# Four instead of three pairs of k-tiles by seven products in the second part's down projections

## The chip, the cores and the metric

The program runs on one core of one Trainium2 chip. The metric is the device time of one execution in microseconds (us). The kernel before has a median of 1944.74 us over 3 runs (1944.4 to 1944.83). A kernel's trace is one further execution, taken by the hardware profiler.

## The reference: one decoder block, of which the two feed-forward networks matter here

```python
def swiglu(x, w_gu, w_down):
    gate, up = jnp.split(x @ w_gu, 2, axis=-1)
    return (jax.nn.silu(gate) * up) @ w_down

h = h + 0.5 * swiglu(rms_norm(h, ffn1_norm[i]), ffn1_w_gu[i], ffn1_w_down[i])
...                                    # the mixer: input projection, DeltaNet, attention, output projection
h = h + 0.5 * swiglu(rms_norm(h, ffn2_norm[i]), ffn2_w_gu[i], ffn2_w_down[i])
...                                    # per-layer embedding, last norm
```

There are 256 tokens (two row tiles of 128, called t = 0 and 1), a model width of 2048 and a hidden width of 5632, all in float32, one layer.

## The kernel before, in words

**Exactness by two halves.** Every float32 operand is split into a rounded part and a rest: ScalarE casts (`whi`, `shi`, `hTh`), VectorE subtracts (`wlo`, `slo`, `hTl`). One product is then three matmuls on TensorE: hi·hi, lo·hi, hi·lo. A 128x512 block of weights for one k-tile and one row tile thus takes three matmuls.

**Parts and groups.** The hidden width is 11 blocks of 512, cut by `PARTS` into a first part of 3 blocks and a second and a third part of 4. For each part the kernel runs one gate/up group per block and then two down groups (`dn`, `nb` = 0 and 2), each of which makes two column blocks of 512 of the down projection. A down group of the second part has 8 pairs of k-tiles in each of its two column blocks. The groups of one feed-forward network are a fixed list (`plan`), and there are two such networks: the first fills the first third of the trace, the second its last two fifths.

**Two ways of multiplying.** In a group some pairs of k-tiles go the plain way: a weight pair is loaded (L74, 512 KB), cast (`whi`, L77), subtracted (`wlo`, L78) and used by 12 matmuls (L550 to L552). The other pairs, `ns` of them for each column block, are multiplied by a Winograd form of Strassen's scheme: the four quarters (two k-tiles by two column blocks) need seven products instead of eight. The class `Group` does this. A quarter is a tile `R` of 128 x (ns·512), loaded by `load` (L279, GpSimd's DMA queue). `all_sums` makes the seven right-hand sides in turn: cast `shi` from `R` (L298, ScalarE), subtract to `slo` (L299, VectorE), and between them add quarters into `R` (L307 on VectorE, or L314, a DMA that adds). `product` uses each with 3·ns matmuls (L342 to L344). I call the seven products of a group p1 to p7, in the order in which they run. After p1 and p2 ScalarE copies the sum to another bank (L347); after p3 and p5 it copies their bank aside (L350) for a VectorE subtraction (L352).

**Buffers.** `shi` and `slo` have two buffers each, `whi` and `wlo` three, `raw` four. The cast of p3 therefore waits until p1 has been multiplied, that of p4 until p2 has been, and so on; a `whi` waits for the pair three before it.

**The left-hand sides.** Four of the seven products use sums of row tiles and k-tiles of the activations. `halves` makes them: for each pair of k-tiles an addition (L456), four additions or subtractions of quarters (L462), a cast `Sh` (L464) and a subtraction `Sl` (L465). In a part after the first it takes one pair at a time, as the hidden blocks come out of `down_input` (which transposes them by way of DRAM).

**What sets the order.** The seven products of a group stand among the plain pairs of the group before it: after one or two plain pairs, one product after each further pair. So the products of the second part's first down group (D1 below) stand in that part's last gate/up group, those of the second down group (D2) among D1's plain pairs, and those of the next gate/up group (ns = 4) among D2's. Within these lists a scheduler orders the instructions of each engine when the program is built; each engine then runs its own list in that order.

**What the change touches:** `NS_DOWN` (L31) with `plan`, `halves`, `ffn` and the weights' layout.

Of the kernel before, what the change touches and what calls it, by code (L numbers as in the profile page):

```python
# [26 lines left out]
PARTS = ((0, 3), (3, 7), (7, 11))  # L27


NS = 4  # L30
NS_DOWN = tuple(3 if i1 - i0 == 4 else 2 for i0, i1 in PARTS)  # L31


SEVEN = (0, 1, 2, 4, 3, 5, 6)
# [12 lines left out]
def block_kernel(ctx, tc, a, out):  # L47
# [306 lines left out]
    def plan(n):  # L354


        def sources(name, blk):

            q, pairs = a[name + "q"][blk], a[name][blk]
            return [q[:, :, g, :].rearrange("j p n -> p j n") for g in range(q.shape[2])] + \  # L360
                [pairs[g] for g in range(pairs.shape[0])], q

        groups = []
        for p, (i0, i1) in enumerate(PARTS):
            for i in range(i0, i1):
                plain = PLAIN[n]
                if i < plain:
                    src = [([a[f"w_gu{n}0"][2 * i + b][g] for g in range(KD // 2)], None) for b in range(2)]
                else:
                    src = [sources("w_gu" + n, 2 * (i - plain) + b) for b in range(2)]  # L370
                groups.append(Group("gu", p, [x[0] for x in src], [x[1] for x in src], NS if i >= plain else 0,
                                    len(groups) % 2))
            for nb in (0, 2):
                src = [sources(f"w_down{n}{p}", nb + b) for b in range(2)]
                groups.append(Group("dn", p, [x[0] for x in src], [x[1] for x in src], NS_DOWN[p], len(groups) % 2, nb))
        if n == "2":
            src = [sources("w_behind", b) for b in range(2)]
            groups.append(Group("behind", len(PARTS), [x[0] for x in src], [x[1] for x in src], NS_BEHIND,
                                len(groups) % 2))
        if n == "1":  # L380

            groups[0].plain.sort(key=lambda x: x[1])
        made, carried = [], []
        for i, group in enumerate(groups):
            group.follower = follower = groups[i + 1] if i + 1 < len(groups) else None
            after = groups[i + 2] if i + 2 < len(groups) else None
            n_plain = len(group.plain)
            at, loads, carried = [], {0: carried}, []
            if follower is not None and follower.ns:
                first = 8 if not group.ns else 4 if follower.kind == "behind" else \  # L390
                    1 if group.kind == follower.kind or group.part and follower.kind == "dn" else 2
                at = [min(first + j, n_plain - 1) for j in range(7)]
                if not group.ns:
                    follower.first = n

                    loads.setdefault(max(at[0] - 5, 0), []).extend(follower.loads())
                if after is not None and after.ns:
                    *three, last = after.loads(follower)
                    for x, one in zip((4, 5, 6), three):
                        loads.setdefault(at[x], []).append(one)  # L400
                    carried = [last]
            todo = []
            for j, (b, g) in enumerate(group.plain):
                todo.append(("plain", (b, g)))
                order.append(("pair", group.src[b][g]))
                if group.kind == "behind" and g == KD // 2 - 1:
                    order.append(("pair", a["w_pp"][b]))
                for x in range(7):
                    if at and at[x] == j:
                        todo.append(("seventh", x))  # L410
                        order.append(("sum", follower))
                order.extend(loads.get(j, []))
            made.append((group, todo))
        return made
# [8 lines left out]
    def halves(kind, his, los, ns, wait=0, at_once=2):  # L423
# [19 lines left out]
        for g0 in range(0, ns, at_once):  # L443
            n = min(at_once, ns - g0)
            k0 = 2 * (g0 % 2)
            hi, lo = (x[g0 // 2][:, k0:k0 + 2 * n] for x in (his, los))
            keep = lambda ins: ins
            if g0 == 2 and n == 1:

                keep = tc.keep_in_program_order  # L450
                yield
            if n == 2:
                x = fp.tile([P, 2 * NB], F32, tag="sil", name="S")
            else:
                x = act.tile([P, NB], F32, tag="nat", name="S", bufs=4)
            keep(nc.vector.tensor_tensor(out=x, in0=hi.bitcast(F32).rearrange("p k x -> p (k x)"),  # L456
                                         in1=lo.bitcast(F32).rearrange("p k x -> p (k x)"), op=ALU.add))
            xv = x.rearrange("p (g j t y) -> p g j t y", g=n, j=2, t=2)
            a11, a12, a21, a22 = (xv[:, :, j, t, :] for t in range(2) for j in range(2))
            for o, y, z, op in ((a22, a21, a22, ALU.subtract), (a21, a11, a21, ALU.subtract),  # L460
                                (a11, a22, a11, ALU.subtract), (a12, a11, a12, ALU.add)):
                nc.vector.tensor_tensor(out=o, in0=y, in1=z, op=op)  # L462
            sx = [y[:, g0:g0 + n].rearrange("p g j t y -> p (g j t y)") for y in (sh, sl)]
            nc.scalar.copy(sx[0], x)  # L464
            nc.vector.tensor_tensor(out=sx[1], in0=x, in1=sx[0], op=ALU.subtract)  # L465
            if not g0 % 2 + n == 1 or g0 + n == ns:
                yield

    def ffn(n, nT, r, scale, next_norm, stat):
        xs = picker(*nT)  # L470
        late = callable(r)
        with tc.tile_pool(name="ffn", bufs=1) as fp:
# [43 lines left out]
            for group, todo in ffn_plan[n]:  # L516
# [5 lines left out]
                if dn and group.nb and not group.last:  # L522
                    lanes.add(1, halves("gu", *nT, NS))
                elif dn and group.nb and group.follower:
                    lanes.add(1, halves("behind", *nxt, NS_BEHIND, 4))
                elif not dn and group.follower.kind == "dn" and not group.part:
                    lanes.add(1, halves("dn", hTh[i0:], hTl[i0:], NS_DOWN[group.part]))
                if dn and group.last and nxt is None:
                    nxt = new_nT()
                if group.banks is None:  # L530
# [1 line left out]
                for kind, one in todo:  # L532
                    if kind == "seventh":
                        follower = group.follower
                        follower.product(SEVEN[one])
                        if group.part and not dn and one == 5 and follower.kind == "gu" and \
                                follower.follower.kind == "dn":
                            p = PARTS[group.part][0]
                            lanes.add(1, halves("dn", Later(hTh, p), Later(hTl, p), NS_DOWN[group.part], 0, 1))
                        continue  # L540
                    b, g = one
                    whi, wlo = next_weights()
# [29 lines left out]
                    else:  # L572
# [7 lines left out]
                        hTl.append(tl)  # L580
                        i0, i1 = PARTS[group.part]

                        last = (3 if i1 - i0 == 4 else 2) if len(hTh) == i1 else 0
                        gen = down_input(outs, sil, th, tl, last)
                        next(gen)

# [762 lines left out]
def _layout(i):  # L1349
# [7 lines left out]
    for n in "12":  # L1357
# [4 lines left out]
        _parted(m, f"w_gu{n}", b[2 * PLAIN[n]:], NS)  # L1362
        b = _blocks(f[f"ffn{n}_w_down"][0])
        for p, (i0, i1) in enumerate(PARTS):
            _parted(m, f"w_down{n}{p}", b[:, 2 * i0:2 * i1], NS_DOWN[p])
    _parted(m, "w_behind", _blocks(f["ple_w_gate"][0])[0:2], NS_BEHIND)
    w = f["w_in"][0]
    m["w_in"] = _blocks(np.concatenate([w[:, :4096], w[:, 4112:]], axis=1))
# [29 lines left out]
```

## Time and profile before

| | |
|---|---|
| median of 3 runs | 1944.74 us |
| profiled execution | 1945.28 us |
| its span, first to last instruction | 1943.6 us |
| mean granted TensorE clock | 0.999 |
| matmuls in the trace | 8884 |
| busy share of the span | TensorE 99%, VectorE 81%, ScalarE 60%, GpSimd 8% |
| a quarter of the second part's down weights | 768 KB, 7.0 us from issue to landing |
| a quarter of the gate/up weights | 1024 KB, 8.3 us |

Times in the trace are counted from the span's start. In lists of groups the columns are the line, the engine, the operation, output and inputs with their shapes, the count, then busy us and mean ns of one, then the idle time of the engine before them with what ended it. In a timeline a row has its start in us, its duration in us, the engine, the line and the operation; an idle time in brackets is the engine's own, and names what ended it. PE is TensorE, PEld its weight loads, DVE VectorE, ACT ScalarE, POOL GpSimd.

### The profile page before, as it was taken

To read this page: it belongs to the slowest core of one execution; us is meant where nothing else is said; L and a number is where in the kernel's file an instruction comes from. 1 tells how busy PE (TensorE), PEld (TensorE's weight loads), DVE (VectorE), ACT (ScalarE), POOL (GpSimd) and SP (SyncE) were. 2 spreads that over 40 slices of the span, in tenths; PEclk is the share of its full clock that TensorE was granted. 3 is DMA by queue.
4 is the path that set the end of the run, shared out by engine and by line. 5 is a ranking of instruction groups with operands and counts; after the bars stand their busy time and mean duration, and the time that the engine had idled before them with its cause. 6 is when DMAs were issued, how large, how long until landed. Compare 5 with 4: busy or idle time off the path is not lost.

```text
span 1943.6 us, 24163 instructions
## 1 busy us (share of the span) xinstructions
PE 1928.1 (99%) x8884; PEld 1594.0 (82%) x8884; DVE 1570.4 (81%) x1703; ACT 1164.1 (60%) x1362; POOL 148.4 (8%) x226
## 2 busy tenths in 40 slices
PE   9999999999999999999999999999999999999998
PEld 7888888888888888878788888888888888888886
DVE  7879878997789766797856579899888987888865
ACT  6656666666666557664555456566556755657654
POOL 0010110000010000010100000010000100001000
PEclk9999999999999999999999999999999999999999
DMA  8778898888888765556565776788888987989764
GB/s 307 269 236 282 252 293 285 237 288 249 280 285 242 228 218 171 176 169 211 161 213 159 244 283 231 226 281 289 248 275 241 327 264 244 271 237 314 234 214 143
DMA packets 144182, 475.05 MB, mean 244 GB/s; under 512 B 19648, under 2 KB 47296, under 8 KB 129856
## 3 DMA queue, kind: packets, MB, share of 16 engines
q1 hardware_dynamic: 107200, 302.16, 44.4%
q0 software_dynamic: 25920, 160.44, 30.2%
q10 hardware_dynamic: 10944, 10.91, 1.8%
q8 instruction: 69, 1.13, 0.2%
q14 instruction: 49, 0.40, 0.1%
HBM read 451.44 MB, written 22.02 MB: 244 GB/s over the span
## 4 chain that ended last, share of the span: by engine, by line
PE 92%; DVE 5%; DMA 2%; issue 1%; ACT 0%; POOL 0%; SPq 0%; POOLq 0%; DVEq 0%; ACTq 0%
PE d L550 5%; PE d L552 5%; PE d L551 5%; PE u L551 5%; PE u L552 5%; PE u L550 5%; PE g L343 5%; PE g L342 5%; PE g L344 5%; PE g L551 4%; PE g L552 4%; PE pj L112 4%; PE pj L113 4%; PE pj L114 4%; PE g L550 4%; PE d L344 3%
## 5 line engine op out<-in xcount | busy, mean ns | idle before, releaser
L77 ACT CAST whi<-raw 128x1024 fp32r<-128x1024 f32 (+1 forms) x489 | 511.3, 1049 | 401.1 <-PE pj L114 106.6
L78 DVE TENSOR_TENSOR wlo<-raw,whi 128x1024 fp32r<-128x1024 f32 (+1 forms) x489 | 592.0, 1218 | 162.9 <-ACT whi L77 161.8
L299 DVE TENSOR_TENSOR slo<-R,shi 128x2048 fp32r<-128x2048 f32 (+2 forms) x224 | 444.9, 1989 | 132.1 <-ACT shi L298 130.1
L298 ACT CAST shi<-R 128x2048 fp32r<-128x2048 f32 (+2 forms) x224 | 373.9, 1671 | 141.5 <-DVE R L307 62.7
L112 PE MATMUL pj<-whi,nTh 128*128 128x512 f32 x448 | 179.4, 401 | 0.0
L113 PE MATMUL pj<-wlo,nTh 128*128 128x512 f32 x448 | 175.2, 391 | 1.1 <-DVE wlo L78 1.1
L114 PE MATMUL pj<-whi,nTl 128*128 128x512 f32 x448 | 174.9, 390 | 0.0
L550 PE MATMUL d<-whi,hTh 128*128 128x512 f32 x448 | 174.5, 390 | 0.0
L551 PE MATMUL d<-wlo,hTh 128*128 128x512 f32 x448 | 174.4, 389 | 0.0
L552 PE MATMUL d<-whi,hTl 128*128 128x512 f32 x448 | 173.4, 389 | 0.0
L551 PE MATMUL g<-wlo,nTh 128*128 128x512 f32 x400 | 156.6, 391 | 0.6 <-DVE wlo L78 0.6
L552 PE MATMUL g<-whi,nTl 128*128 128x512 f32 x400 | 156.0, 390 | 0.0
L551 PE MATMUL u<-wlo,nTh 128*128 128x512 f32 x400 | 155.8, 389 | 0.2 <-DVE wlo L78 0.2
L552 PE MATMUL u<-whi,nTl 128*128 128x512 f32 x400 | 155.6, 389 | 0.0
L550 PE MATMUL g<-whi,nTh 128*128 128x512 f32 x400 | 155.0, 391 | 0.6 <-ACT nTh L161 0.6
L550 PE MATMUL u<-whi,nTh 128*128 128x512 f32 x400 | 153.4, 389 | 0.0
L307 DVE TENSOR_TENSOR R<-R 128x2048 f32<-128x2048 f32 (+2 forms) x68 | 135.7, 1996 | 0.1
L113 PEld LDWEIGHTS pj<-wlo,nTh 128*128 128x128 f32 x448 | 84.2, 188 | 18.9 <-DVE wlo L78 2.7
L550 PEld LDWEIGHTS d<-whi,hTh 128*128 128x128 f32 x448 | 84.1, 188 | 18.1 <-ACT hTh L504 1.0
L552 PEld LDWEIGHTS d<-whi,hTl 128*128 128x128 f32 x448 | 84.1, 188 | 17.8
L114 PEld LDWEIGHTS pj<-whi,nTl 128*128 128x128 f32 x448 | 84.1, 188 | 17.6
L551 PEld LDWEIGHTS d<-wlo,hTh 128*128 128x128 f32 x448 | 84.1, 188 | 17.4
(332 smaller groups left out, 3447.0 us busy)
## 6 DMA issues: line engine op xcount, KB each, us to landing
raw<-in_w_gu SPq DMA_DIRECT2D x199, 512.0 KB, 5.8
raw<-in_w_down SPq DMA_DIRECT2D x112, 512.0 KB, 6.4
raw<-in_w_in SPq DMA_DIRECT2D x112, 512.0 KB, 3.4
R<-in_w_gu2q POOLq DMA_DIRECT2D x54, 1024.0 KB, 8.6
R<-in_w_gu1q POOLq DMA_DIRECT2D x48, 1024.0 KB, 8.3
raw<-in_w_out SPq DMA_DIRECT2D x32, 512.0 KB, 4.3
tT<-scr SPq DMA_DIRECT2D x22, 512.0 KB, 5.8
R<-in_w_down11q POOLq DMA_DIRECT2D x12, 768.0 KB, 7.0
```

The source lines that it names most:

```text
L77: nc.scalar.copy(hi[:, j, :], raw[:, j, :])
L78: nc.vector.tensor_tensor(out=lo[:, j, :], in0=raw[:, j, :], in1=hi[:, j, :], op=ALU.subtract)
L112: nc.tensor.matmul(outs[t], xh[:, c], whi[:, j, :], start=st, stop=False)
L113: nc.tensor.matmul(outs[t], xh[:, c], wlo[:, j, :], start=False, stop=False)
L114: nc.tensor.matmul(outs[t], xl[:, c], whi[:, j, :], start=False, stop=sp)
L298: keep(nc.scalar.copy(hi, w))
L299: nc.vector.tensor_tensor(out=lo, in0=w, in1=hi, op=ALU.subtract)
L307: keep(nc.vector.tensor_tensor(out=self.raw[x], in0=self.raw[x], in1=self.raw[y], op=ALU.add))
L344: nc.tensor.matmul(out, xl, whi[:, g, :], start=False, stop=sp, skip_group_check=True)
L550: nc.tensor.matmul(out, xh[:, c], whi[:, j, :], start=st, stop=False, skip_group_check=True)
L551: nc.tensor.matmul(out, xh[:, c], wlo[:, j, :], start=False, stop=False, skip_group_check=True)
L552: nc.tensor.matmul(out, xl[:, c], whi[:, j, :], start=False, stop=sp, skip_group_check=True)
```

## The change

Each of the four down groups of the second part (two in each network) takes 4 instead of 3 pairs by seven products, and 4 instead of 5 of each column block the plain way. The first part stays at 2, the third at 3. The table now has one entry for each of a part's two down groups, and each has its own weight tensors.

```diff
-NS_DOWN = tuple(3 if i1 - i0 == 4 else 2 for i0, i1 in PARTS)
+NS_DOWN = (2, 2), (4, 4), (3, 3)
...
             for nb in (0, 2):
-                src = [sources(f"w_down{n}{p}", nb + b) for b in range(2)]
-                groups.append(Group("dn", p, [x[0] for x in src], [x[1] for x in src], NS_DOWN[p], len(groups) % 2, nb))
+                src = [sources(f"w_down{n}{p}{nb // 2}", b) for b in range(2)]
+                groups.append(Group("dn", p, [x[0] for x in src], [x[1] for x in src], NS_DOWN[p][nb // 2],
+                                    len(groups) % 2, nb))
...
-            if g0 == 2 and n == 1:
+            if g0 >= 2 and n == 1:
 
                 keep = tc.keep_in_program_order
-                yield
+                if g0 == 2:
+                    yield
...
-                    lanes.add(1, halves("dn", hTh[i0:], hTl[i0:], NS_DOWN[group.part]))
+                    lanes.add(1, halves("dn", hTh[i0:], hTl[i0:], NS_DOWN[group.part][0]))
...
-                            lanes.add(1, halves("dn", Later(hTh, p), Later(hTl, p), NS_DOWN[group.part], 0, 1))
+                            lanes.add(1, halves("dn", Later(hTh, p), Later(hTl, p), NS_DOWN[group.part][0], 0, 1))
...
-                        last = (3 if i1 - i0 == 4 else 2) if len(hTh) == i1 else 0
+                        last = (6 - NS_DOWN[group.part][0] if i1 - i0 == 4 else 2) if len(hTh) == i1 else 0
...
-            _parted(m, f"w_down{n}{p}", b[:, 2 * i0:2 * i1], NS_DOWN[p])
+            for j in range(2):
+                _parted(m, f"w_down{n}{p}{j}", b[2 * j:2 * j + 2, 2 * i0:2 * i1], NS_DOWN[p][j])
```

The scheduler's order moves with it. In the changed kernel, lines after L375 count one to three higher. Numbers behind a name are those of a tile's allocation; a tile that is the same in both programs need not have the same number.

The first place is VectorE in the last gate/up group of the second part, first network, from the hidden block that the halves need (`hTl_2383`) to the second plain pair after p1 (`wlo_2749`). Before:

```order
L505 TENSOR_TENSOR hTl_2383<-tT_2604,hTh_2382 128x4x4x32 x2
L299 TENSOR_TENSOR slo_2728<-R_2548,shi_2727 128x1536
L487 STREAM_TRANSPOSE tb_2744<-sil_2526 128x4x128
L307 TENSOR_TENSOR R_2548<-R_2548,R_2625 128x1536
L487 STREAM_TRANSPOSE tb_2744<-sil_2526 128x4x128
L78 TENSOR_TENSOR wlo_2749<-raw_2747,whi_2748 128x1024
L456 TENSOR_TENSOR S_2770<-hTh_2382,hTl_2383 128x512
L299 TENSOR_TENSOR slo_2793<-R_2548,shi_2792 128x1536
```

The same engine and place in the changed kernel:

```order
L507 TENSOR_TENSOR hTl_2383<-tT_2604,hTh_2382 128x4x4x32 x2
L78 TENSOR_TENSOR wlo_2711<-raw_2709,whi_2710 128x1024
L299 TENSOR_TENSOR slo_2728<-R_2548,shi_2727 128x2048
L489 STREAM_TRANSPOSE tb_2744<-sil_2526 128x4x128
L307 TENSOR_TENSOR R_2548<-R_2548,R_2625 128x2048
L489 STREAM_TRANSPOSE tb_2744<-sil_2526 128x4x128
L78 TENSOR_TENSOR wlo_2749<-raw_2747,whi_2748 128x1024
L458 TENSOR_TENSOR S_2770<-hTh_2382,hTl_2383 128x512
L299 TENSOR_TENSOR slo_2804<-R_2548,shi_2803 128x2048
```

p2's subtraction and the second addition are 2048 wide in place of 1536, and the first plain pair's `wlo_2711` has moved from before `hTl_2383` to behind it.

The second place is TensorE at the end of the same gate/up group, among D1's products p4 to p7 (`d` is a down bank, `u` a bank of the gate/up group). Before, p5 (`shi_2862`) and p6 (`shi_2895`) have plain matmuls of the group's last pair (`whi_2902`) between them:

```order
L344 MATMUL d1_2779<-shi_2862,Sl_2684 128x512
L551 MATMUL u0_2453<-wlo_2903,nTh_102 128x512
L342 MATMUL d0_2780<-shi_2895,Sh_2683 128x512
L552 MATMUL u0_2453<-whi_2902,nTl_106 128x512
L550 MATMUL u1_2454<-whi_2902,nTh_102 128x512
L551 MATMUL u1_2454<-wlo_2903,nTh_102 128x512
```

In the changed kernel the last plain pair (`whi_2922`) ends where p4 (`shi_2839`) and p5 (`shi_2879`) begin:

```order
L342 MATMUL d0_2786<-shi_2839,hTh_2085 128x512
L552 MATMUL u1_2454<-whi_2922,nTh_102 128x512
L553 MATMUL u1_2454<-wlo_2923,nTh_102 128x512
L554 MATMUL u1_2454<-whi_2922,nTl_106 128x512
L342 MATMUL d1_2787<-shi_2879,Sh_2683 128x512
L343 MATMUL d0_2786<-slo_2840,hTh_2085 128x512
L344 MATMUL d0_2786<-shi_2839,hTl_2086 128x512
```

After the last of these rows the remaining matmuls of p4, p5, p6 (`shi_2915`) and p7 (`shi_2956`), 44 of them, follow each other with no plain matmul among them; before, 12 plain matmuls (all those of `whi_2902`) stand among p4 to p7.

The third place is ScalarE in the changed kernel beside it, behind the copy (L347) that waits for p2's end:

```order
L298 CAST shi_2839<-R_2633 128x2048
L350 COPY part_2876<-d1_2787 128x512
L298 CAST shi_2879<-R_2584 128x2048
L77 CAST whi_2983<-raw_2982 128x1024
L77 CAST whi_3035<-raw_3034 128x1024
L298 CAST shi_2915<-R_2625 128x2048
```

Before, three casts of plain weights stand at the place of these two, and the casts of `R` are 1536 wide. The second network's list has the same pattern.

## The prediction

> **What bounds the kernel now.** I read the page's first parts, then TensorE's waits, then the groups by shape, then the timeline around D1.
>
> ```profile
> span 1943.6 us, 24163 instructions
> PE 1928.1 (99%) x8884; PEld 1594.0 (82%) x8884; DVE 1570.4 (81%) x1703; ACT 1164.1 (60%) x1362; POOL 148.4 (8%) x226
> PE 92%; DVE 5%; DMA 2%; issue 1%; ACT 0%; POOL 0%; SPq 0%; POOLq 0%; DVEq 0%; ACTq 0%
> ```
>
> TensorE is busy for 99% of the span and is 92% of the chain that ended last. A busy share can hide gaps, so the waits come next (totals of the whole run: us, times, longest).
>
> ```profile
> PE vp L1129 <- DVE R L1150: 1.2, 1, 1.2
> PE pj L113 <- DVE wlo L78: 1.1, 3, 0.5
> ...
> PE u L343 <- DVE slo L299: 0.3, 1, 0.3
> PE u L551 <- DVE wlo L78: 0.2, 1, 0.2
> ```
>
> In the feed-forward networks TensorE waits for almost nothing: for `slo` 0.3 us in all. So every matmul taken out is worth its full time, and every wait that comes in costs its full time. What decides is whether VectorE and ScalarE stay ahead around D1. Two stretches there (us, then PE, PEld, DVE, ACT, POOL busy, clock, DMA):
>
> ```profile
> 340.00:350.00 10.00, 10.00 (x45) 8.27 (x45) 10.00 (x19) 6.24 (x8) 0.89 (x1) 1.00 0.68 150
> 380.00:390.00 10.00, 10.00 (x46) 8.28 (x45) 10.00 (x11) 6.49 (x7) 0.89 (x1) 1.00 0.86 220
> ```
>
> VectorE's 81% is an average. Here it is at 10.00 of 10, and the question is how far ahead of TensorE it runs.
>
> **The change part by part.** The durations by shape:
>
> ```profile
> L78 DVE TENSOR_TENSOR wlo<-raw,whi 128x1024 fp32r<-128x1024 f32 x487 | 590.6, 1220 | 160.2 <-ACT whi L77 159.1
> L299 DVE TENSOR_TENSOR slo<-R,shi 128x2048 fp32r<-128x2048 f32 x133 | 304.4, 2290 | 112.7 <-ACT shi L298 111.9 <-DMA raw<-in_w_gu 0.6
> L298 ACT CAST shi<-R 128x2048 fp32r<-128x2048 f32 x133 | 254.3, 1913 | 104.1 <-DVE R L307 53.7 <-PE g L344 27.2 <-PE u L344 21.2
> L299 DVE TENSOR_TENSOR slo<-R,shi 128x1536 fp32r<-128x1536 f32 x56 | 97.9, 1754 | 10.3 <-ACT shi L298 10.1
> L307 DVE TENSOR_TENSOR R<-R 128x2048 f32<-128x2048 f32 x42 | 95.7, 2280 | 0.1
> L298 ACT CAST shi<-R 128x1536 fp32r<-128x1536 f32 x56 | 83.0, 1482 | 21.9 <-PE d L344 8.4 <-PE g L344 6.8 <-PE u L344 6.7
> L307 DVE TENSOR_TENSOR R<-R 128x1536 f32<-128x1536 f32 x16 | 27.9, 1746 | 0.0
> ```
>
> *What is saved.* One pair in each of two column blocks was 24 plain matmuls and becomes 21. Four groups save 12. The next rows give a matmul's pace: from 346.40 to 353.45 TensorE starts 31 (9 of p1, 12 of a plain pair, 6 of p2, 4 of the next pairs), so 0.227 us each. The saving is 12 × 0.227 = 2.7 us, 1.36 in each network.
>
> ```profile
> 346.40 0.39 PE L342 MATMUL d<-shi,hTh 128*128 128x512 f32 x1
> 353.45 0.50 PE L551 MATMUL g<-wlo,nTh 128*128 128x512 f32 x1
> ```
>
> *What the other engines get.* For each network VectorE's 14 subtractions grow by 2.290 − 1.754 = 0.54 us and its 4 additions by 0.53, four `wlo` of 1.22 go, and one more pair of halves comes (about 2 us): 7.5 + 2.1 − 4.9 + 2 = +6.7 us. ScalarE's 14 casts grow by 0.43 each. TensorE's time shrinks. If all this lay in idle time, it would cost nothing; the idle time is elsewhere.
>
> *First place: the second plain pair after p1.* VectorE before:
>
> ```profile
> 337.23 1.76 DVE L299 TENSOR_TENSOR slo<-R,shi 128x1536 fp32r<-128x1536 f32 x1 [0.50 <-ACT shi L298]
> 340.98 0.69 DVE L456 TENSOR_TENSOR S<-hTh,hTl 128x512 f32<-128x512 f32 x1
> 341.58 0.90 DVE L462 TENSOR_TENSOR S<-S 128x128 f32<-128x128 f32 x4
> 349.95 1.73 DVE L307 TENSOR_TENSOR R<-R 128x1536 f32<-128x1536 f32 x1
> 351.58 0.71 DVE L487 STREAM_TRANSPOSE tb<-sil 128x512 f32<-128x512 f32 x1
> 352.21 1.19 DVE L78 TENSOR_TENSOR wlo<-raw,whi 128x1024 fp32r<-128x1024 f32 x1
> ```
>
> From p1's subtraction at 337.23 VectorE runs without idle time to this `wlo`, which ends at 352.21 + 1.19 = 353.40. TensorE uses it at 353.45: the lead is 0.05 us. With the change p1's cast takes 0.43 longer, two subtractions and two additions in this stretch are 0.54 longer each (2.14), and one addition of the halves (0.60, the step from 340.98 to 341.58) moves ahead of p1's subtraction, into its wait for the cast. The `wlo` then starts at 352.21 + 0.42 + 2.14 − 0.60 = 354.17 and ends at 355.39. TensorE has three more matmuls in p1 and wants it at 346.40 + 34 × 0.227 = 354.12. **The wait is 1.3 us.** Its bounds are 0, if VectorE's queue had slack that the rows don't show, and 2.1, if the addition finds no room.
>
> Right behind it, p3's subtraction and the next `wlo` stand in the same queue:
>
> ```profile
> 353.91 1.76 DVE L299 TENSOR_TENSOR slo<-R,shi 128x1536 fp32r<-128x1536 f32 x1
> 355.78 1.23 DVE L78 TENSOR_TENSOR wlo<-raw,whi 128x1024 fp32r<-128x1024 f32 x1
> ...
> 356.10 0.39 PE L343 MATMUL d<-slo,Sh 128*128 128x512 f32 x1
> 357.23 0.39 PE L551 MATMUL u<-wlo,nTh 128*128 128x512 f32 x1
> ```
>
> Their leads are 356.10 − 355.67 = 0.43 and 357.23 − 357.01 = 0.22 us, and p3's subtraction is again 0.54 longer with a cast 0.43 longer ahead of it. I take 0.5 us, between 0 and 1.0. TensorE runs its list in order, so nothing behind a waiting matmul passes it.
>
> *Second place: p4 to p7 without plain matmuls among them.* `shi` has two buffers, so p5's cast waits for p3's end and p6's for p4's. What this loop takes, before the change:
>
> ```profile
> 361.96 0.57 ACT L347 COPY d<-d 128x512 f32<-128x512 f32 x1 [0.33 <-PE d L344]
> 362.44 1.48 ACT L298 CAST shi<-R 128x1536 fp32r<-128x1536 f32 x1
> 363.82 0.58 ACT L350 COPY part<-d 128x512 f32<-128x512 f32 x1
> 364.30 1.49 ACT L298 CAST shi<-R 128x1536 fp32r<-128x1536 f32 x1
> 368.11 0.39 PE L344 MATMUL d<-shi,hTl 128*128 128x512 f32 x1
> 368.54 1.48 ACT L298 CAST shi<-R 128x1536 fp32r<-128x1536 f32 x1
> 370.17 1.75 DVE L299 TENSOR_TENSOR slo<-R,shi 128x1536 fp32r<-128x1536 f32 x1
> 372.87 0.39 PE L343 MATMUL d<-slo,Sh 128*128 128x512 f32 x1
> ```
>
> The last matmul of p4 ends at 368.50, p6's cast starts at 368.54, its subtraction ends at 371.92, and TensorE wants it at 372.87: 0.95 us of lead, because plain matmuls lie between. In the changed order they don't.
>
> p5: behind p2's last matmul come, on ScalarE, the copy (0.48 to the next start), p4's cast (1.91 − 0.10), the second copy (0.48) and p5's cast (1.91). With the matmul's 0.39 and 0.08 for two hand-overs this is 5.15 us. In the changed order TensorE has 17 matmuls, 3.86 us, from p2's last matmul to p5's first, which stands ahead of p4's remaining 11 and holds them up: **1.3 us**.
>
> p6: behind p4's last matmul (0.39) come its cast (1.91 and 0.03) and its subtraction (2.29 and 0.03), 4.65 us. TensorE has p5's 11 and p6's first matmul, 13 steps, 2.95 us: a wait of at least 1.6. VectorE also has a `wlo` and the two gating products between (1.1 + 2 × 0.66), which hold the subtraction some 0.3 longer. I take **1.9**; the bounds are 1.6 and 2.3. p7 then finds its buffer free almost two microseconds longer, and I take 0.1 us for it, and 0.1 for p5's own subtraction. Sum of this place: 3.4.
>
> *Third place: D2's p3 and p4.* They are neighbours as well, and p4's cast stands on ScalarE behind p3's, which waits for VectorE's second addition. Laid on from the places above, that addition ends some 0.6 us too late. I take 0.6, between 0 and 0.9.
>
> *What I cost at nothing.* A quarter of 1024 KB lands later than one of 768:
>
> ```profile
> R<-in_w_gu1q POOLq DMA_DIRECT2D x48, 1024.0 KB, 8.3
> R<-in_w_down11q POOLq DMA_DIRECT2D x12, 768.0 KB, 7.0
> ```
>
> D2's first quarter is fetched once p4's subtraction has ended and is cast when p5 and p6 have been multiplied, about 10 us later, so 8.3 us are covered; without that cover each group would lose up to 1.3. Eight weight pairs fewer are loaded; the third part's order is unchanged.
>
> *The sum.* For each network 1.3 + 0.5 + 3.4 + 0.6 = 5.8 us of waits, less 1.36: +4.45. Both networks have the same order there, so +8.9. The profiled execution took 1945.28 us (its span and 1.7 around it); with the change 1954.2. It lies 0.54 above the runs' median, so for a median I take 1944.74 + 8.9 = **1953.6 us**.
>
> **The rivals.**
>
> *Only TensorE's own work counts* (the other side). VectorE is idle for a fifth of the run and ScalarE for two fifths; if in this stretch they got ahead by as much as they do elsewhere, the waits would vanish and 1944.74 − 2.7 = 1942.0 us would come out, no change that can be told. The place is the same pair of `shi` buffers: it decides if p4's and p5's casts begin 1.3 us earlier than laid out, and p6's 1.9. Against it stands the lead of 0.05 us at 353.40, and that a cast can't begin before its buffer is free. Chance 0.10. The Trainium skill's Perfetto Trace Analysis, section Identifying the Most-Contended Engine, says that occupancy is a fair measure of how close VectorE is to its limit and that the engine with the highest one is to be improved first. By that rule, with VectorE at 81%, the sum would be the saving alone; the stretches at 10.00 of 10 speak against using the average.
>
> *The buffer loop alone.* If VectorE's queue has more slack than I see, the first and third places cost nothing: 3.4 − 1.36 = 2.04 in each network, 1944.74 + 4.1 = 1948.8. For it: the loop needs nothing but matmul, cast and subtraction times. Against it: the lead of 0.05. Chance 0.25.
>
> *VectorE stays late into the next gate/up group.* D2 shrinks from 204 matmuls with its seventh products (46.3 us) to 180 (40.9), and VectorE's 8 `wlo`, 7 subtractions and 2 additions there are 9.8 + 16.0 + 4.6 = 30.4, with the next halves and the updates of `h` on top. If it doesn't catch up, 2 us more in each network: 1957.6. Chance 0.15.
>
> *That the change does something else* can be left aside: the built order has 12 matmuls fewer and D1's and D2's `slo` at 2048.
>
> **How the numbers follow.** The forecast has 0.50. A measurement of this kernel can tell about 0.2%, 3.9 us, from no change. Slower by more: the forecast and the late VectorE, 0.65, and 0.6 of the loop alone (its 4.1 lies just above the bound), 0.15: 0.80. Within: the rest of that, 0.10, and most of the first rival, 0.08: 0.18. Faster by more: at most 2.7 us are saved, so 0.02 for what I overlook. The range, 1946 to 1958.5, leaves out the first rival and the far ends of the waits.
>
> **What would show it.** In the changed profile TensorE's waits should list `slo` (L299), `shi` (L298) and `wlo` (L78) in down groups, some 6 us in each network, single ones of 1 to 2 us in front of p5 and p6, and none in the third part. The count of matmuls should fall by 12. If the waits are there without those at `wlo`, the buffer loop alone was right; if TensorE shows no wait of more than 0.5 us in D1, my laying out of the casts is wrong.

## The result, and the profile after

| | before | changed |
|---|---|---|
| median | 1944.78 us, 4 runs (1944.4 to 1945.01) | 1958.55 us, 4 runs (1958.07 to 1960.61) |
| ratio, 95% interval | | 1.0073 (1.0059 to 1.0087) |
| profiled execution, span | 1945.28, 1943.6 us | 1958.07, 1956.2 us |

The change makes the kernel 13.8 us slower. The forecast was 1953.6 us: the side is right, the loss is 5 us larger than forecast, and the median lies just above the upper end of the range, 1958.5.

The first parts of the changed kernel's page:

```profile
span 1956.2 us, 24111 instructions
PE 1929.8 (99%) x8872; PEld 1590.1 (81%) x8872; DVE 1585.8 (81%) x1707; ACT 1169.9 (60%) x1356; POOL 148.9 (8%) x226
PE 88%; DVE 7%; DMA 2%; issue 1%; ACT 1%; POOL 0%; SPq 0%; ACTq 0%; POOLq 0%; DVEq 0%
```

The matmuls are 12 fewer, as they should be, and the shares of busy time are what they were. The chain that ended last has moved: TensorE has 88% of it instead of 92%, VectorE 7% instead of 5%. TensorE's waits of the whole run (total us, times, longest) say where:

```profile
PE d L342 <- ACT shi L298: 3.4, 4, 1.1
PE d L343 <- DVE slo L299: 3.2, 2, 1.6
PE d L342 <- ACT Sh L466: 3.0, 2, 1.6
PE g L553 <- DVE wlo L78: 2.9, 4, 1.1
...
PE at L1243 <- DVE st L1236: 0.7, 1, 0.7
```

Three of the first four lines were forecast. The third was not: `Sh` is a cast of the halves. The timeline of the first network around D1 shows each wait as an idle time in brackets behind TensorE's row, and what released it; between them stand the rows of four other queues that lead to the wait at 369.17:

```profile
355.11 0.50 PE L553 MATMUL g<-wlo,nTh 128*128 128x512 f32 x1 [1.15 <-DVE wlo L78]
355.45 0.39 PE L554 MATMUL g<-whi,nTl 128*128 128x512 f32 x1
355.68 0.40 PE L553 MATMUL g<-wlo,nTh 128*128 128x512 f32 x1
...
358.16 0.88 POOL L314 DMA_DIRECT2D R<-in_w_down110q  x1 [14.92 <-DVE S L464]
...
359.26 1.67 SPq L74 DMA_DIRECT2D raw<-in_w_down  x2
...
365.08 0.28 DVE L464 TENSOR_TENSOR S<-S 128x128 f32<-128x128 f32 x1
...
367.55 1.04 ACT L77 CAST whi<-raw 128x1024 fp32r<-128x1024 f32 x1 [2.78 <-DMA raw<-in_w_down]
368.50 0.61 ACT L466 CAST Sh<-S 128x512 fp32r<-128x512 f32 x1
369.17 0.50 PE L342 MATMUL d<-shi,Sh 128*128 128x512 f32 x1 [1.45 <-ACT Sh L466]
...
375.84 0.50 PE L342 MATMUL d<-shi,Sh 128*128 128x512 f32 x1 [1.10 <-ACT shi L298]
...
383.34 0.50 PE L343 MATMUL d<-slo,Sh 128*128 128x512 f32 x1 [1.64 <-DVE slo L299]
...
406.35 0.50 PE L342 MATMUL d<-shi,hTh 128*128 128x512 f32 x1 [0.58 <-ACT shi L298]
```

To compare them with the forecast I count the time from one matmul's start to the next beyond the pace of 0.227 us (0.2267 in the sums). Row by row this gives 1.31 at the second plain pair's `wlo` (355.11), 0.18 at p3's `slo`, **1.61 at the fourth quarter's `Sh` (369.17)**, 1.27 at p5, 1.80 at p6 (383.34) and 0.74 at D2's p4 (406.35). The matmul behind a waiting one starts 0.34 us after it instead of 0.227 (355.11 to 355.45; 0.23 again to 355.68): a restart of 0.11 for nearly every wait.

Added up over all matmul starts from 335 to 465 us these gaps are 8.66 us, and from 1480 to 1600 us, in the second network, 8.79; before, 0.47 and 0.50. So the sum closes: 1944.78 − 12 × 0.227 + (17.45 − 0.97) = 1958.5 us, against 1958.55 measured.

How the missed wait comes about stands in the middle of the fence. With four quarters of halves instead of three, one more cast `Sh` stands in ScalarE's queue. What it casts is ready when VectorE's addition at 365.08 ends, at 365.36, but in the queue the cast of D1's first plain pair stands ahead of it. That pair's load (the first of the two in its row) was issued at 359.26, one microsecond behind the adding DMA of 1024 KB (L314, 358.16), and took 8.2 us to land. So the `Sh` cast begins at 368.50, 3.1 us after its data were there. The load's row in the list of issues, with its size and the us from issue to landing:

```profile
raw<-in_w_down SPq DMA_DIRECT2D x1, 512.0 KB, 8.2
```

Before the change the same load was nearly as slow, but the last `Sh` cast of the halves, at 358.91, stood well ahead of the cast that waits for it:

```profile
raw<-in_w_down SPq DMA_DIRECT2D x1, 512.0 KB, 7.8
```

```profile
358.91 0.62 ACT L464 CAST Sh<-S 128x512 fp32r<-128x512 f32 x1 [5.08 <-DVE S L462]
```

So the change did not bring the slow load; it put a cast that TensorE needs behind it.

### The profile page after: what moved, and what is told of

Same layout as the page of the kernel before. It is cut to its first block, busy times and chain, and to the rows that moved or that the text cites. A ratio compares the mean times of both kernels' runs of the same rounds, so it can differ in the third digit from the quotient of the medians.

```text
span 1956.2 us, 24111 instructions
## 1 busy us (share of the span) xinstructions
PE 1929.8 (99%) x8872; PEld 1590.1 (81%) x8872; DVE 1585.8 (81%) x1707; ACT 1169.9 (60%) x1356; POOL 148.9 (8%) x226
## 4 chain that ended last, share of the span: by engine, by line
PE 88%; DVE 7%; DMA 2%; issue 1%; ACT 1%; POOL 0%; SPq 0%; ACTq 0%; POOLq 0%; DVEq 0%
PE d L552 5%; PE d L553 5%; PE d L554 5%; PE g L343 4%; PE g L342 4%; PE g L344 4%; PE u L554 4%; PE u L553 4%; PE u L552 4%; PE pj L112 4%; PE pj L113 4%; PE pj L114 4%; PE g L553 4%; PE g L554 4%; PE g L552 4%; PE d L343 3%
## 5 line engine op out<-in xcount | busy, mean ns | idle before, releaser
L77 ACT CAST whi<-raw 128x1024 fp32r<-128x1024 f32 (+1 forms) x481 | 503.1, 1050 | 390.9 <-PE pj L114 110.3
L78 DVE TENSOR_TENSOR wlo<-raw,whi 128x1024 fp32r<-128x1024 f32 (+1 forms) x481 | 582.1, 1216 | 162.7 <-ACT whi L77 161.5
L299 DVE TENSOR_TENSOR slo<-R,shi 128x2048 fp32r<-128x2048 f32 (+2 forms) x224 | 459.7, 2055 | 125.4 <-ACT shi L298 122.9
L298 ACT CAST shi<-R 128x2048 fp32r<-128x2048 f32 (+2 forms) x224 | 386.0, 1724 | 149.4 <-DVE R L307 72.0
L552 PE MATMUL d<-whi,hTh 128*128 128x512 f32 x416 | 162.1, 390 | 0.0
L553 PE MATMUL d<-wlo,hTh 128*128 128x512 f32 x416 | 161.9, 389 | 0.0
L554 PE MATMUL d<-whi,hTl 128*128 128x512 f32 x416 | 160.9, 389 | 0.0
L112 PEld LDWEIGHTS pj<-whi,nTh 128*128 128x128 f32 x448 | 84.2, 188 | 16.7
L553 PEld LDWEIGHTS g<-wlo,nTh 128*128 128x128 f32 x400 | 75.1, 188 | 21.1 <-DVE wlo L78 5.5
L552 PEld LDWEIGHTS d<-whi,hTh 128*128 128x128 f32 x416 | 78.1, 188 | 17.0 <-ACT hTh L506 1.0
```

Of the source, the lines that this page charges most:

```text
L77: nc.scalar.copy(hi[:, j, :], raw[:, j, :])
L78: nc.vector.tensor_tensor(out=lo[:, j, :], in0=raw[:, j, :], in1=hi[:, j, :], op=ALU.subtract)
L112: nc.tensor.matmul(outs[t], xh[:, c], whi[:, j, :], start=st, stop=False)
L298: keep(nc.scalar.copy(hi, w))
L299: nc.vector.tensor_tensor(out=lo, in0=w, in1=hi, op=ALU.subtract)
L552: nc.tensor.matmul(out, xh[:, c], whi[:, j, :], start=st, stop=False, skip_group_check=True)
```

## The experiments

Theory A: the waits are separate. Each has its own cause (VectorE's queue at `wlo`, the late load in front of the quarter's cast, the loop of the two `shi` buffers at p5, p6 and D2's p4), and the time is the sum of the gaps. Theory B: VectorE has too much to do around the two groups as a whole, and what is eased in one place comes out at the next. Rival C: the buffer loop alone.

### One group at a time

```diff
-NS_DOWN = (2, 2), (4, 4), (3, 3)
+NS_DOWN = (2, 2), (4, 3), (3, 3)      # D1 alone
+NS_DOWN = (2, 2), (3, 4), (3, 3)      # D2 alone; the halves are made for max(3, 4)
```

> Only D1 takes four pairs by seven products; D2 stays at three. Theory A: nearly all the loss is D1's (waits of 1.3, 0.2, 1.6, 1.3 and 1.8 us and 0.1 behind each), D2's part is one wait of 0.75 against a saving of 0.68: 1958.2 us. Theory B: the extra work of VectorE is shared by both groups (6.7 us in each network), so half of the waits go: 1951 to 1953 us.

> Only D2 takes four pairs by seven products; D1 stays at three (the fourth quarter of the halves is still made, for D2). Six matmuls fewer in all, 1.36 us. Theory A (separate waits): D1 has no waits, as before; D2 has at most the one wait of 0.75 and its restart of 0.1 in each network: between 1944.8 - 1.4 = 1943.4 us and 1945.1 us. Theory B (VectorE's work as a whole): about half of the loss, 1951 us.

D1 alone: 1958.46 us, ratio 1.0070 (1.0058 to 1.0083), with D1's waits all there and the one in D2 gone. D2 alone: 1942.45 us over 11 runs, ratio 0.9988 (0.9979 to 0.9997), and no wait is listed in either network around the two groups; its page:

```profile
span 1941.4 us, 24133 instructions
PE 1925.8 (99%) x8878; PEld 1592.4 (82%) x8878; DVE 1579.9 (81%) x1711; ACT 1166.8 (60%) x1360; POOL 148.9 (8%) x226
```

Theory B is out: the same kind of extra work costs 13.7 us in D1 and nothing in D2. And even the fourth quarter of the halves, which this kernel also makes, costs nothing while D1's products don't need it. VectorE's share is 81% here, 81% before and 81% in the kernel that is 16 us slower. Where the Trainium skill's Perfetto Trace Analysis, section Identifying the Most-Contended Engine, takes an engine's occupancy for its closeness to the limit, these three runs show that the average doesn't tell them apart.

### The buffer loop: operands in two pieces

```diff
-                keep(nc.scalar.copy(hi, w))
-                nc.vector.tensor_tensor(out=lo, in0=w, in1=hi, op=ALU.subtract)
+                for c in self.cuts: keep(nc.scalar.copy(hi[:, c], w[:, c]))
+                for c in self.cuts: nc.vector.tensor_tensor(out=lo[:, c], in0=w[:, c], in1=hi[:, c], op=ALU.subtract)
```

In D1 and D2 `cuts` are pairs 0 to 1 and 2 to 3; elsewhere it is one piece.

> The cast to shi and the subtraction to slo of D1 and D2 are done in two pieces of two pairs each, so a product can begin when half of its operand is there. The loop from a buffer's release to the next matmul shrinks by a cast of two pairs (about 0.95 us) for p5 and by that and half a subtraction (about 2.1 us) for p6; VectorE and ScalarE have as much to do as before, and a little more for 14 extra instructions each per group pair. Theory A: the wait at p5 falls from 1.3 to 0.3 us, that at p6 from 1.8 to 0, that of D2's p4 from 0.75 to 0; 3.7 us less in each network with the restarts: 1951 us. The waits at wlo and at the fourth quarter's cast stay. Theory B: VectorE's work as a whole sets the time; no gain, 1958.5 us or up to 1961.

1946.84 us over 11 runs, ratio 1.0011 (1.0003 to 1.002): 11.7 us of the 13.8 are gone. The groups by shape, then what is left of waits in down groups:

```profile
L299 DVE TENSOR_TENSOR slo<-R,shi 128x1024 fp32r<-128x1024 f32 x91 | 108.5, 1220 | 11.4 <-ACT shi L298 10.3
L298 ACT CAST shi<-R 128x1024 fp32r<-128x1024 f32 x91 | 93.0, 1050 | 32.1 <-DVE R L307 19.7 <-PE u L344 5.6 <-PE d L344 4.8
```

```profile
PE d L554 <- DVE hTl L507: 0.8, 2, 0.4
PE d L342 <- ACT shi L298: 0.8, 2, 0.4
...
PE g L553 <- DVE wlo L78: 0.6, 2, 0.4
```

VectorE and ScalarE are as busy as in the changed kernel, and p5, p6 and D2's p4 wait no more. But the pieces are not the only difference: the order moved too. Here p5's first matmul stands behind p4's twelve instead of ahead of eleven of them, and behind p4's second matmul six plain matmuls stand among p4 to p7, where the changed kernel has none. As an estimate from this trace's rows, with whole operands in this order p4's first matmul would still have waited some 0.8 us (its cast starts at 368.15, takes 1.91, and is wanted at 369.29) and p6 some 0.6 (p4's last matmul starts at 372.89, the loop is 4.65, and p6 is wanted at 376.99). By this estimate the pieces are worth about 1.4 of the 3.1 us that went at p5 and p6, and the order the rest.

The gain is 4.3 us larger than expected, and 3.6 of this is the wait for the quarter, which went as well: p3's subtraction now ends later, so the adding DMA behind it is issued at 362.95, after the weight load, which is cast at 364.78, and `Sh` follows at 365.74. What is left in a network, about 1 us at p3's `shi` and at `wlo` behind VectorE's additions and 0.57 at `hTl`, is VectorE's queue, the forecast's first place.

Two half measures were meant to tell p5's cast from p6's subtraction:

> Only the cast to shi is done in two pieces in D1 and D2; the subtraction to slo stays whole; p4 to p7 stand back to back as in the changed kernel. Theory A: p5 waits for a cast, and its wait falls from 1.3 to 0.3 us; p6 waits for a subtraction, which still needs both pieces, and stays at 1.8; D2's p4 waits for a cast, 0.75 falls to 0: 1958.55 - 2 x (0.95 + 0.75 + 0.1) = 1954.9 us, with the waits at wlo and at the fourth quarter's cast unchanged. If the casts alone are the whole loop: 1947 to 1950 us. Theory B: 1958.5 us.

> Only the subtraction to slo is done in two pieces in D1 and D2; the cast to shi stays whole. In D1 the matmuls stand almost as in the changed kernel, p4 to p7 back to back and as many plain matmuls ahead of p5. Theory A: p5 waits for a cast and stays at 1.3 us; p6 waits for the subtraction, of which the first piece takes 1.22 instead of 2.29 us, so 1.8 falls to about 0.7; the waits at wlo and at the fourth quarter's cast stay: 1958.55 - 2 x 1.1 = 1956.3 us. Theory B (VectorE's work as a whole): 1958.5 us or more.

Neither came out as expected, since the scheduler made another order of each. The cast in pieces took 1962.67 us, ratio 1.009 (1.0077 to 1.0104), slower than the changed kernel. In its order only two plain matmuls are left between p3's end and p5's first one, where there had been fourteen. Twelve matmuls of cover are 2.7 us; the first piece of a cast is ready only 0.9 us sooner. Its timeline there (TensorE's rows, from p4's first matmul on):

```profile
373.42 0.50 PE L342 MATMUL d<-shi,hTh 128*128 128x512 f32 x1 [0.94 <-ACT shi L298]
375.79 0.49 PE L342 MATMUL d<-shi,Sh 128*128 128x512 f32 x1 [1.88 <-ACT shi L298]
...
378.39 0.63 PE L343 MATMUL d<-slo,hTh 128*128 128x512 f32 x1
378.82 0.63 PE L344 MATMUL d<-shi,hTl 128*128 128x512 f32 x1
...
381.59 0.39 PE L343 MATMUL d<-slo,Sh 128*128 128x512 f32 x1
381.82 0.39 PE L344 MATMUL d<-shi,Sl 128*128 128x512 f32 x1
```

The two gaps are 1.10 and 2.15 us, 2.0 more than the 1.27 in the changed kernel, as 2.7 − 0.9 would have it; and then the matmuls themselves are slow, 0.43 us apart: more on that at the end. The subtraction in pieces took 1950.75 us, ratio 1.0032 (1.0019 to 1.0044), 5.5 us faster than expected. In its order p5's first matmul stands behind p4's twelve (p4's first waits 1.31 in the first network and not in the second, p5 in neither), p6's wait is gone, and on ScalarE the `Sh` cast stands ahead of the late one:

```profile
365.36 0.62 ACT L466 CAST Sh<-S 128x512 fp32r<-128x512 f32 x1 [0.62 <-DVE S L464]
368.72 1.05 ACT L77 CAST whi<-raw 128x1024 fp32r<-128x1024 f32 x1 [2.74 <-DMA raw<-in_w_down]
```

So the share of the cast and that of the subtraction were not separated. Both runs agree with the loop, in that a wait is its length less the matmuls that the order puts into it; how much of p6's wait is the cast's and how much the subtraction's stays open.

### The first place: VectorE's queue before `wlo`

```diff
-                keep(nc.vector.tensor_tensor(out=self.raw[x], in0=self.raw[x], in1=self.raw[y], op=ALU.add))
+                x, y, z = (self.raw[q][:, :3 if self.kind == "dn" and self.ns == 4 and not self.nb else self.ns] for q in (x, x, y)); keep(nc.vector.tensor_tensor(out=x, in0=y, in1=z, op=ALU.add))
```

> D1's two additions on VectorE take three of the four pairs of columns, so the fourth pair's sums are wrong; all else is as in the changed kernel. 2 x 0.53 us of VectorE's work ahead of the first wait are gone. Theory A and B: the wait at the second plain pair's wlo falls from 1.3 us to about 0.25, us for us, and everything behind moves up: 1958.55 - 2 x 1.05 = 1956.4 us. Rival C (the buffer loop alone): the time stays at 1958.5. A case in between: the gain at wlo is given back at the fourth quarter's cast, whose weight load does not come earlier; then 1958.5 with a longer wait there.

1957.26 us, ratio 1.0067 (1.0054 to 1.0079). In the trace the gap at `wlo` is 0.25 us in both networks, as expected: VectorE was late there us for us, and rival C is out. The time fell by 1.3 us and not by 2.1, and the runs of one kernel are as far apart, so it is the gap that shows the cause. In the first network 0.13 came back at p3; in the second a wait of 1.25 us appeared in D2 that the changed kernel's first trace doesn't have, for `hTh` (L506), the cast of the hidden block that D2 still lacks.

### The wait for the fourth quarter

Two kernels take it away, one by its cause and one by the queue. The first leaves out the adding DMA:

```diff
-                nc.gpsimd.dma_start(out=self.raw[x], in_=self.quarters[y[1]][y[0]], accum_op=ALU.add)
+                if not (self.kind == "dn" and self.part == 1 and not self.nb and x == (0, 0)): nc.gpsimd.dma_start(out=self.raw[x], in_=self.quarters[y[1]][y[0]], accum_op=ALU.add)
```

> Leaves out one of D1's two adding transfers, the second (1024 KB, issued just ahead of the weight load that the fourth quarter's cast ends up behind), so the sums of p4 to p7 lack one term; every engine's order is the same. Theory A (separate waits, each with its own cause): the wait of 1.6 to 1.7 us for the cast of the fourth quarter of the halves comes from a weight load that lands late behind this transfer; with the transfer gone it goes, with 0.1 us of restart, in both networks: 1958.55 - 2 x 1.75 = 1955.0 us, and the waits at p5 and p6 stay at 1.3 and 1.8. Theory B (VectorE has too much to do as a whole, and a wait only shows where TensorE runs into its lateness): the lateness comes out at p5 instead and the time stays at 1958.5. Rival C (only the loop of the two shi buffers counts): 1958.5 as well, with the wait for the quarter unchanged.

> The kernel that leaves out D1's second adding transfer (so the sums of p4 to p7 lack one term) once more, because its first runs spread from 1956.96 to 1960.87 us while its trace showed 1.6 us less of waits in the first network and 0.9 less in the second. If the time follows the waits in the networks: 1958.6 - 1.6 - (0.9 to 1.7), 1955.3 to 1956.1 us. If something outside them takes it back each time: 1958 us, and the stretch between the networks is longer by 1 to 2 us than in the changed kernel.

```profile
366.17 1.05 ACT L77 CAST whi<-raw 128x1024 fp32r<-128x1024 f32 x1 [1.20 <-issue]
367.12 0.62 ACT L466 CAST Sh<-S 128x512 fp32r<-128x512 f32 x1
```

```profile
raw<-in_w_down SPq DMA_DIRECT2D x1, 512.0 KB, 3.1
```

These are ScalarE's rows in the first of the two runs, and the same load's row in the list of issues. The load, issued at 359.45, now takes 3.1 us to land instead of 8.2 (3.1 in the second run too). The cast of its pair, at 366.17, no longer waits for a transfer, and the wait for `Sh` is gone in both networks of both runs, while the gaps at p5 and p6 stay at 1.26 and 1.76. So the late load behind the adding DMA is its cause. But the time hardly moved: 1958.06 us, ratio 1.0076 (1.0063 to 1.009), and again 1957.83, 1.0067 (1.0053 to 1.008). Where it went shows in the second of the two runs, by its waits and by D2's timeline:

```profile
PE d L552 <- ACT hTh L506: 2.3, 2, 1.2
PE at L1243 <- DVE st L1236: 1.8, 1, 1.8
```

```profile
401.33 0.33 SPq L500 DMA_DIRECT2D tT<-scr  x1
...
407.59 1.14 ACT L506 CAST hTh<-tT 128x512 fp32r<-128x512 f32 x2 [2.67 <-DMA tT<-scr]
```

and the same place in the changed kernel, run once more beside other experiments:

> The changed kernel once more, beside the others on the same chip: 1958.5 us, and the same waits (1.3 at wlo, 0.2, 1.6 to 1.7 at the fourth quarter's cast, 1.3 at p5, 1.8 at p6, 0.75 at D2's p4).

```profile
403.46 0.33 SPq L500 DMA_DIRECT2D tT<-scr  x1
...
407.98 1.14 ACT L506 CAST hTh<-tT 128x512 fp32r<-128x512 f32 x2 [0.93 <-DMA tT<-scr]
```

TensorE and the transposed block's transfer both come 2.1 us earlier, but the transfer takes 6.3 us instead of 4.5, so its data are only 0.4 us earlier, and TensorE waits 1.35 us for them. In the first of the two runs the same transfer took 4.5 us and TensorE did not wait for it there, so its length varies from execution to execution. The wait at `hTh` is the next limit in D2. The changed kernel meets it too at times: this repeat (1958.65 us, ratio 1.0074, 1.0061 to 1.0086, with all the listed waits) has it in its second network, 1.0 us, and the first trace has not. The other line, `at`, is a wait in the attention between the networks: 1.8 us in both runs without the adding DMA, 0.6 to 0.7 in the changed kernel, the repeat and the two-pieces kernel. Why leaving out this DMA should lengthen it I can't say; it stays open.

The second kernel leaves nothing out. It begins the last quarters one step earlier and keeps the `Sh` cast at its place in the program:

```diff
-                if g0 == 2:
+                if g0 == 2 and ns == 3:
                     yield
...
-            nc.scalar.copy(sx[0], x)
+            (keep if ns == 4 else lambda q: q)(nc.scalar.copy(sx[0], x))
```

> The halves' third and fourth quarters are begun one step earlier and the fourth quarter's cast stands in ScalarE's queue ahead of the cast of D1's first plain pair, whose load lands late; nothing is left out. On VectorE one addition of 0.60 us and one of 0.2 move ahead of the first wlo and p3's subtraction. Theory A: the wait for the quarter, 1.6 to 1.7 us and its restart, goes; the wait at wlo grows by 0.6 to 1.9 and the one at p3 by 0.2; p5 and p6 stay: 1958.55 - 2 x 0.9 = 1956.7 us. Theory B: the lateness comes out at p5, 1958.5 to 1960 us.

ScalarE's rows, and TensorE's waits from 330 to 465 us:

```profile
364.68 0.62 ACT L466 CAST Sh<-S 128x512 fp32r<-128x512 f32 x1 [0.63 <-DVE S L464]
367.17 1.05 ACT L77 CAST whi<-raw 128x1024 fp32r<-128x1024 f32 x1 [1.86 <-PE d L343]
```

```profile
PE d L342 <- ACT shi L298: 2.2, 3, 1.4
PE d L343 <- DVE slo L299: 1.6, 1, 1.6
```

1953.88 us, ratio 1.0052 (1.0038 to 1.0065): 4.8 us less than the repeat beside it. The wait for the quarter is gone, as expected, and p6's 1.79 stands unchanged. The gain is more than the 1.8 us expected mostly because in this order p5's first matmul no longer stands in front of p4's: a gap of 0.44 in place of 1.27. The first place comes out at 1.68 us, where I expected 1.9.

### A faster version?

With D2 alone in pieces, and with both groups in pieces and `Sl` moved to GpSimd:

```diff
-            nc.vector.tensor_tensor(out=sx[1], in0=x, in1=sx[0], op=ALU.subtract)
+            (nc.gpsimd if kind == "dn" and ns == 4 else nc.vector).tensor_tensor(out=sx[1], in0=x, in1=sx[0], op=ALU.subtract)
```

> As the run with D2 alone, and D2's casts and subtractions in two pieces. Theory A: no wait in either group, 1943.4 us. If the fourth quarter of the halves by itself costs something, 1944 to 1946 us.

> As the run with both groups in two pieces, and the subtractions to Sl (128x512, 0.68 us on VectorE, four in each network) are done by GpSimd in the second part's down groups. What is left there, per network, is 0.55 at p2's shi, 0.42 at the second plain pair's wlo and 0.2 of restarts. Theory A: both come from VectorE's queue, two Sl subtractions (0.60 each to the next start) stand ahead of them, and they go: 1946.84 - 2 x 1.2 = 1944.4 us, if GpSimd is about as fast (its select of 128x512 takes 0.87 us in the changed kernel). If GpSimd takes several microseconds, p2 waits for Sl and it is 1947 to 1952 us. Rival: what is left does not come from VectorE, 1946.8 us.

The first took 1943.18 us, ratio 0.9991 (0.9982 to 1.0000): D2 alone has no wait left that pieces could shorten. The second took 1950.44 us, ratio 1.0029 (1.0017 to 1.004), 3.6 us slower than without GpSimd. TensorE's waits, then GpSimd's and VectorE's timeline where the first two subtractions run:

```profile
PE d L344 <- DVE hTl L507: 2.8, 2, 1.4
PE d L344 <- POOL Sl L467: 1.8, 2, 0.9
```

```profile
344.35 1.29 POOL L467 TENSOR_TENSOR Sl<-S,Sh 128x512 fp32r<-128x512 f32 x1 [1.53 <-ACT Sh L466]
...
344.69 1.10 DVE L464 TENSOR_TENSOR S<-S 128x128 f32<-128x128 f32 x1
...
346.52 1.56 POOL L467 TENSOR_TENSOR Sl<-S,Sh 128x512 fp32r<-128x512 f32 x1 [0.88 <-ACT Sh L466]
...
346.85 2.32 DVE L299 TENSOR_TENSOR slo<-R,shi 128x1024 fp32r<-128x1024 f32 x1
```

VectorE was spared 0.60 us for each of these two subtractions and lost more, 0.8 and 1.1 us, on the instructions that ran beside GpSimd's: L464 alone takes 0.28 us and L299 on 1024 columns 1.22. The order moved as well: this piece of `slo`, with 1.1 us of its own, stands ahead of `hTl`, and in the two-pieces kernel it stands behind. So `hTl` came 1.4 us late instead.

The version that beats both kernels is D2 alone. Its gain is 0.12% with an interval of 0.03% to 0.21%, less than the 0.2% that the prediction set as the bound.

### The sum of the gaps against the time

In each row the time from the gaps is 1944.78 − 0.227 × (matmuls fewer) + (gaps of both networks − 0.97), with the gaps from one trace.

| kernel | matmuls fewer | gaps, us | from the gaps | median |
|---|---|---|---|---|
| changed | 12 | 17.45 | 1958.5 | 1958.55 |
| changed, repeated | 12 | 18.58 | 1959.7 | 1958.65 |
| D1 alone | 6 | 16.29 | 1958.7 | 1958.46 |
| D2 alone | 6 | 0.40 | 1942.8 | 1942.45 |
| D2 alone, two pieces | 6 | 0.82 | 1943.3 | 1943.18 |
| two pieces | 12 | 5.81 | 1946.9 | 1946.84 |
| two pieces, GpSimd | 12 | 9.47 | 1950.6 | 1950.44 |
| cast in pieces | 12 | 21.79 | 1962.9 | 1962.67 |
| subtraction in pieces | 12 | 10.33 | 1951.4 | 1950.75 |
| quarter's cast first | 12 | 13.74 | 1954.8 | 1953.88 |
| short additions | 12 | 16.92 | 1958.0 | 1957.26 |
| no adding DMA | 12 | 14.88 | 1956.0 | 1958.06 |
| no adding DMA, again | 12 | 17.10 | 1958.2 | 1957.83 |

Twelve of thirteen agree within 1.1 us, so nearly all of every difference lies in the gaps around these two groups. Most of the gaps are TensorE standing still; in the kernel with only the cast in pieces, 1.6 and 1.5 us of them are slow matmuls. The row that doesn't agree, 2.1 us off, is the first run without the adding DMA: its trace is of an execution of 1956.96 us, 1.1 under the median, and the longer wait in the attention is another 1.1.

## Why the prediction was right and where it was wrong

- **That waits decide, and not TensorE's own work.** Right. The saving is the forecast 12 matmuls, and the waits outweigh it six times over.
- **First place.** Forecast 1.3 and, behind it, 0.5; measured 1.31 and 0.6. The second agreement is partly luck: p3's own wait was 0.18, and the rest are restarts, which the forecast didn't have, and a little at the next `wlo`. The short additions showed the cause: 1.06 us less on VectorE, 1.06 us less of wait.
- **Second place.** Forecast 1.3 for p5 and 1.9 for p6; measured 1.27 and 1.80. The cast in pieces, with twelve matmuls of cover fewer, made the waits up to p5's first matmul larger by 2.0 where the loop gives 1.8. The two-pieces kernel removes both with VectorE as busy as before, by the pieces and by its order together. (For p6 the forecast's own sum, 4.65 − 2.95, gives 1.7, not the 1.6 that it took as the lower bound; nothing hangs on it.)
- **Third place.** Forecast 0.6, measured 0.74; gone with D1 alone and with two pieces.
- **The step that failed is the list of what I cost at nothing.** It went through the loads of the quarters and the third part, and the change's extra pair of halves came in only as an addition on VectorE. Its cast on ScalarE, for which p2 and p3 wait, was not laid out: in ScalarE's list it stands behind the cast of a weight pair, and that pair lands 8.2 us after its issue. That is 1.61 and 1.74 us in the two networks, 3.4 us in all. The quarter's cast put first is 4.8 us faster, and the part beyond these 3.4 is mostly p5's.
- **The restart** of 0.11 us behind a wait was left out as well, though two rows before the change show it in the first network (353.79 and 436.28 us). After the change there are ten such rows in each network, eight more, about 0.9 us. With the quarter's wait this makes up the 4.9 us that the forecast lacked: 1.61 + 1.74 + about 1.8 = 5.1, and what the other terms were off by nearly cancels.
- **The rivals.** "Only TensorE's own work counts" fell with the waits in the trace, "the buffer loop alone" with the short additions, and "VectorE late into the next gate/up group" because no wait is listed from 409 to 465 us. "The change does something else" was rightly set aside. None of the rivals was the missed one.
- **The range** ended at 1958.5 because each term's bounds were taken from rows of that term. It had no room for a term that was not in the list.

## What to carry to other kernels

When an operation is added to an engine that is not the bottleneck, lay out that engine's whole queue in the place: what stands ahead of the new instruction, and whether any of that waits for a transfer. A loop of two buffers costs its length less the independent work that the order puts between, so operands handed over in two pieces can win some of it back, and the order that is made when the program is built can win or lose as much. A saving on the busiest engine is best tried group by group: here one of two equal-looking groups carried the whole loss.

## What the runs showed of the hardware

**A thin stretch slows TensorE's clock.** In the kernel with only the cast in pieces, busy time of PE, PEld, DVE, ACT and POOL, granted clock and DMA in two stretches:

```profile
372.00:376.00 4.00, 1.19 (x5) 0.43 (x3) 2.53 (x3) 4.00 (x6) 0.00 (x0) 1.00 1.03 422
378.00:381.00 3.00, 3.00 (x9) 2.35 (x8) 2.57 (x2) 0.23 (x1) 0.56 (x1) 0.50 0.90 298
```

TensorE was busy for 1.19 of 4 us, and then eight matmuls started 0.43 us apart, between 378.0 and 381.4, at a granted clock of 0.50; this cost 1.6 us, and the second network shows it again (1.5 us). In the changed kernel, whose waits of 1.3 to 1.8 us stand some 7 us apart, the granted clock stays at 1.00. The Trainium skill's TensorE: Matmul & The Clock Gate, section What's actually happening, says that the clock falls to half after an idle window of about 3.4 us. The trace agrees on the half; but the stretch ahead of it was not idle, since two matmuls started in it, at 373.42 and 375.79.

**GpSimd's tensor operations hold VectorE up.** The rows above (1.10 in place of 0.28 us, 2.32 in place of 1.22) show VectorE's instruction ending 0.15 us behind GpSimd's (345.79 and 345.64), or about its own length behind it (349.17 and 348.08). The Trainium skill's SBUF — State Buffer, section SBUF: two separate sides, says that the two share a pair of ports that is locked for a whole instruction; the trace agrees.

**A matmul that waited is followed 0.34 us later, not 0.227.** Nearly every wait in every trace shows this restart.
